# Weight loads in 8 KB doubles, the projection moved to the fifth block, and a reordered last block

## The chip, the cores and the metric

The kernel runs on one core of one Trainium2 chip. The metric is the time of one execution on the device in microseconds (us), as the median of several runs. PE is the matrix engine (PEld its weight loads), DVE the vector engine, ACT the activation engine, POOL the general-purpose engine and SP the engine whose queue issues nearly all transfers. The core has 16 DMA engines, which all queues share.

## The reference, cut to what matters

256 tokens of width 1024 pass one hybrid layer, all in 32-bit floats:

```
h = rms_norm(x); proj = h @ w_in                # 1024 x 6160
y_a = attention(q, k, v) @ w_out_a
y_b = state_space_mixer(z, xbc, dt) @ w_out_b
x = x + (gate_a * y_a + gate_b * y_b) @ w_out
h2 = rms_norm(x)
for e in 16 experts:                            # each token uses 2 of them
    he = silu(h2 @ w_gate[e]) * (h2 @ w_up[e])  # 1024 x 512 each
    x += combine[:, e] * (he @ w_down[e])       # 512 x 1024
x = x + sigmoid(x @ w_ple_gate) * (p @ w_ple_proj)
out = rms_norm(x)
```

The weights are 143.6 MB of reads in all; the experts alone hold 16 x 6 MB. Which experts serve which tokens is known only after the router has seen the normalized x.

## The kernel before, in words

**Order of the work.** The input projection, attention, the state-space mixer and the output projections come first (a list of "pieces", each with a split of a weight chunk into a high and a low part, products and an evacuation). Then the router runs (`route`, L998), and the experts are handled in six blocks (`for pr in range(NB)`, L1475): blocks 0 to 3 hold two experts with 64 slots each, blocks 4 and 5 hold four experts with 32 slots each. Experts 0 to 3 (blocks 0 and 1) are always in place, so their weights can be loaded ahead; the experts of the later blocks are taken in an order that `sort_experts` (L1061) writes into registers, and their loads wait for that. A block computes gate and up products (`gate_up`, L1151), transposes the hidden rows (`hidden_T`, L1184), multiplies by the down weights (`down`, L1190), splits the result into yh and yl and adds it back to the tokens one block later (`scatter`, L1208). `down` for the last two blocks is cut in halves and quarters of the output columns (`half_down` L1450, `q_down` L1463), so that the gate `w_ple_gate` (chunks pg_0 to pg_7, `pg_split` L1548, `pg` L1552) can begin on the first columns while the others are still loaded. From L1602 on the order of this last part is written out by hand.

**Memory.** On-chip memory is a ring of 51 units, each 1024 floats (4 KB) in each of 128 partitions (`UNITS`, L20). Activations take units (`Act`, L117; `Late` takes them on first use), and so do weights. A load is 512 KB, one unit. All loads stand in one list, `pending`, in the order of their use, and `pump` (L153) issues as many of its first entries as there is room for, always from SP's queue. `consumed` (L164) gives a weight's unit back when its last product has been issued, and pumps again. `Ring.may` (L73) is the planner: the kernel is first walked through dry, which notes every taking and giving back in program order; a load is admitted if at no point up to its own release the ring would be over-full. A unit that is reused is guarded by a wait of SP's queue on its last reader.

**Rows.** One load brings to each partition rows of contiguous memory: 4 KB for gate and up weights (`w_rows`, L226: two rows of 512 floats of the 8 that a partition holds) and for the down weights of blocks 0 to 3 (`d_rows`, L231), 2 KB for the halves of the down weights in blocks 4 and 5 (`d_half`), 1 KB for their quarters (`d_cols`) and for the input projection's chunks.

**The projection p @ w_ple_proj.** Its input `pin` (256 KB, rows of 1 KB) and its weights `pj_0`, `pj_1` (512 KB each) stand in the list behind w_out, ahead of the experts (L218). `pp_T` transposes p in the output projection's pieces, `pp_fill` strews the products over the places where PE would wait during routing and block 0, and `pp_end` (L1330) evacuates four PSUM banks into two units behind block 0's gate and up products.

Of the kernel before, what the change touches and what calls it, by code (L numbers as in the profile page):

```python
# [15 lines left out]
P = 128  # L16
# [3 lines left out]
UNITS = 51  # L20
# [32 lines left out]
class Ring:  # L53
# [19 lines left out]
    def may(self, name):  # L73
# [3 lines left out]
        if any(self.used[t] >= UNITS for t in r):  # L77
            return False
# [14 lines left out]
def emit(ctx, tc, ring, x, p, mix_norm_g, w_in, conv_w, conv_b, dt_bias,  # L93
# [12 lines left out]
    free = list(range(UNITS))  # L106
    pending, ready = [], {}
    known, regs = [], {}
    dry = ring.used is None

    def unit(name, dt=F32):
        if dry:
            return tc, 0
        i = free.pop(0)
        return big.tile([P, 1024], dt, tag=f"s{i}", name=name), i

    class Act:  # L117
        def __init__(self, name, n, dt=F32):
            ring.note(n)
            got = [unit(f"{name}{j}", dt) for j in range(n)]  # L120
            self.t = [g[0] for g in got]
            self.i = [g[1] for g in got]
# [4 lines left out]
        def free(self, fill=True):  # L127
            ring.note(-len(self.i))
            free.extend(self.i)
            if fill:  # L130
                pump()

    class Late:


        def __init__(self, name, n, dt=F32):
            self.name, self.dt, self.a = name, dt, [None] * n
            self.t = self

        def __getitem__(self, j):  # L140
            if self.a[j] is None:
                self.a[j] = Act(f"{self.name}{j}", 1, self.dt)
# [9 lines left out]

    def pump(limit=None):  # L153
        while pending and limit != 0 and (dry or known or not callable(pending[0][1])) and ring.may(pending[0][0]):
            name, src, nk = pending.pop(0)
            if callable(src) and not dry:
                src = src()
            t, i = unit(name)
            o = t[:, :512] if name == "pin" else t
            sp.dma_start(o.rearrange("p (k f) -> p k f", k=nk), src)  # L160
            ready[name] = (t if name == "pin" else t.rearrange("p (k f) -> p k f", k=nk), i)
# [56 lines left out]
    queue_proj()  # L218
# [7 lines left out]
    def w_rows(x, src, c):  # L226
        if x < FIXED:
            return dram(src, x * D * DFF + 2 * c * DFF, [[KD * DFF, P], [DFF, 2], [1, DFF]])
        return lambda: expert(x, src).rearrange("o (p k) f -> p (o k) f", p=P)[:, 2 * c:2 * c + 2, :]

    def d_rows(x, c):  # L231
        if x < FIXED:
            return rows(w_down, x * D * DFF + c * P * D, 1, D, D)
        return lambda: expert(x, w_down)[:, c * P:(c + 1) * P, :].rearrange("o p d -> p o d")

    def d_half(x, h, o):

        return lambda: expert(x, w_down).rearrange("o (k p) d -> p (o k) d", p=P)[:, 2 * h:2 * h + 2, o:o + 512]
# [1461 lines left out]
```

## Time and profile before

| what | value |
|---|---|
| time, median of 3 runs | 499.83 us (496.88 to 500.16) |
| profiled execution, its own time | 496.42 us |
| span of the profiled execution | 494.4 us |
| granted PE clock over the span | 0.979 of full speed |
| PE busy | 462.0 us (93%) |
| DVE, ACT, POOL busy | 208.5, 183.2, 122.9 us |
| DMA | 73,270 packets, 145.25 MB, mean 294 GB/s |

The span runs from the first to the last instruction of the program; the time around it is the launch. A share of the DMA engines over 1 means that packets overlap a little. "Landing" is when the last byte of a transfer is confirmed. PE's matmuls are pipelined, so a busy PE need not be at its peak.

### The profile page before, as it was taken

Reading aid. Unit: us, or ns where it says so; the run is one execution under the profiler, and the core shown is the slowest. Engines: PE = TensorE matmul, PEld = TensorE weight load, DVE = VectorE, ACT = ScalarE, POOL = GpSimd, SP = SyncE. Lnnn points to the kernel's source line nnn. Section 1 sums busy time; section 2 is a strip of 40 time slices with the busy share of each in tenths; the row PEclk is TensorE's granted clock in tenths of the full one; section 3 lists DMA queues with packets and bytes.
Section 4 is the critical chain, followed back from the end, with each engine's and each line's share of the span. In section 5 each row is a group of like instructions: output and inputs, shape, how many; then the busy total and the mean of one; then the engine's idle time right before and its main releaser. Section 6 shows DMA issues by size and latency. Waiting matters only on the chain.

```text
span 494.4 us, 8088 instructions
## 1 busy us (share of the span) xinstructions
PE 462.0 (93%) x3001; PEld 318.7 (64%) x3001; DVE 208.5 (42%) x412; ACT 183.2 (37%) x333; POOL 122.9 (25%) x82
## 2 busy tenths in 40 slices
PE   7999999999999999999999999999999598879881
PEld 6997998999988999988854354353532121236551
DVE  4424678795669584753635112010110000024345
ACT  5646576634677364443532111020110000123233
POOL 3857546333788630041400000000000000000001
PEclk8999999999999999999999999999999889999997
DMA  8899999611323698769558999999999999999902
GB/s 287 242 335 349 348 349 281 195 61 56 117 85 129 216 397 286 273 200 351 183 189 308 385 410 408 410 409 409 409 409 391 406 407 409 396 396 372 371 35 86
DMA packets 73270, 145.25 MB, mean 294 GB/s; under 512 B 8244, under 2 KB 41352, under 8 KB 73224
## 3 DMA queue, kind: packets, MB, share of 16 engines
q1 hardware_dynamic: 73080, 144.15, 81.1%
q8 instruction: 25, 0.41, 0.3%
q10 hardware_dynamic: 144, 0.52, 0.3%
q14 instruction: 21, 0.17, 0.1%
HBM read 143.61 MB, written 1.05 MB: 293 GB/s over the span
## 4 chain that ended last, share of the span: by engine, by line
PE 72%; DMA 17%; DVE 6%; ACT 2%; issue 1%; POOL 0%; POOLq 0%; DVEq 0%; SPq 0%; ACTq 0%
PE g L1168 7%; DMA u<-in_w_up_dram 6%; PE y L1198 6%; PE u L1168 6%; PE ac_gb L411 5%; PE ac_ob L411 5%; PE ac_ga L411 5%; DMA d_h<-in_w_down_dram 4%; DMA g<-in_w_gate_dram 4%; PE ac_xs L411 3%; PE ac_q L411 2%; PE ac_bc L411 2%; PE ac_z L411 2%; PE g L1111 2%; PE ac_k L411 2%; DMA pg<-in_w_ple_gate_dram 2%
## 5 line engine op out<-in xcount | busy, mean ns | idle before, releaser
L1586 POOL TENSOR_TENSOR stat<-stat,nhalf 128x1 f32<-128x1 f32 x2 | 1.6, 818 | 244.4 <-DVE stat L1581 242.5
L1168 PE MATMUL u<-u,XT 128*64 128x512 f32 (+1 forms) x256 | 55.9, 598 | 3.3 <-DMA u<-in_w_up_dram 3.2
L1168 PE MATMUL g<-g,XT 128*64 128x512 f32 (+1 forms) x256 | 50.4, 643 | 5.7 <-PEq L1245 4.6
L1168 PEld LDWEIGHTS u<-u,XT 128*64 128x64 f32 (+1 forms) x256 | 14.3, 123 | 40.5 <-issue 21.4
L1168 PEld LDWEIGHTS g<-g,XT 128*64 128x64 f32 (+1 forms) x256 | 14.6, 130 | 38.8 <-issue 31.0
L1198 PE MATMUL y<-d,mid 128*64 128x512 f32 x128 | 28.3, 595 | 0.0
L1181 DVE SCALAR_TENSOR_TENSOR mid<-u,cwt,mid 128x512 f32<-128x512 f32 x6 | 4.5, 751 | 50.7 <-issue 49.5
L380 POOL TENSOR_TENSOR wl_xs<-xs,wh_xs 128x1024 fp32r<-128x1024 f32 x8 | 19.2, 2396 | 17.7 <-ACT wh_xs L377 7.8
L1144 ACT ACTIVATE sT<-st 128x256 fp32r<-128x256 f32 x6 | 2.3, 385 | 52.9 <-DVE cwt L1143 50.5
L1205 DVE SCALAR_TENSOR_TENSOR yl<-y,cwt,yh 128x512 fp32r<-128x512 f32 x8 | 6.0, 750 | 34.0 <-ACT yh L1204 33.6
L1140 DVE COPY cwt<-st 128x1 f32<-128x1 f32 x6 | 0.9, 158 | 45.2 <-PE st L1135 45.2
L1198 PEld LDWEIGHTS y<-d,mid 128*64 128x64 f32 x128 | 8.9, 137 | 16.7 <-issue 15.4
L759 POOL TENSOR_TENSOR su<-su,su 128x768 f32<-128x768 f32 x8 | 16.9, 2109 | 7.6 <-ACT su L758 7.0
L1188 ACT ACTIVATE mid<-hT 128x512 f32<-128x512 f32 x5 | 3.0, 598 | 34.7 <-PE hT L1187 34.7
L380 POOL TENSOR_TENSOR wl_wo<-wo,wh_wo 128x1024 fp32r<-128x1024 f32 x3 | 7.8, 2615 | 31.0 <-ACT wh_wo L377 29.6
L389 PE MATMUL pg<-wh_pg,x2h 128*128 128x512 f32 x32 | 13.5, 423 | 0.7 <-ACT x2h L1543 0.7
L1204 ACT ACTIVATE yh<-y,cwt 128x512 fp32r<-128x512 f32 x8 | 5.5, 688 | 22.5 <-PE y L1198 22.5
L380 POOL TENSOR_TENSOR wl_z<-z,wh_z 128x1024 fp32r<-128x1024 f32 x4 | 9.6, 2405 | 16.3 <-ACT wh_z L377 7.1
L390 PE MATMUL pg<-wl_pg,x2h 128*128 128x512 f32 x32 | 12.9, 402 | 0.1
L391 PE MATMUL pg<-wh_pg,x2l 128*128 128x512 f32 x32 | 12.8, 401 | 0.0
L1119 ACT ACTIVATE XT<-g,gfd 128x256 f32<-128x256 f32 x12 | 5.0, 471 | 21.0 <-PE g L1111 21.0
L1111 PE MATMUL g<-S,h2h 128*128 128x256 f32 x44 | 11.5, 295 | 0.6 <-ACT XT L1119 0.6
(413 smaller groups left out, 1169.8 us busy)
## 6 DMA issues: line engine op xcount, KB each, us to landing
g<-in_w_gate_dram SPq DMA_DIRECT2D x64, 512.0 KB, 10.1
u<-in_w_up_dram SPq DMA_DIRECT2D x64, 512.0 KB, 10.1
d<-in_w_down_dram SPq DMA_DIRECT2D x40, 512.0 KB, 9.5
d_h<-in_w_down_dram SPq DMA_DIRECT2D x16, 512.0 KB, 10.4
xs<-in_w_in_dram SPq DMA_DIRECT2D x8, 512.0 KB, 8.7
z<-in_w_in_dram SPq DMA_DIRECT2D x8, 512.0 KB, 8.7
ga<-in_w_in_dram SPq DMA_DIRECT2D x8, 512.0 KB, 8.7
gb<-in_w_in_dram SPq DMA_DIRECT2D x8, 512.0 KB, 6.7
```

The lines of the kernel that those rows point to most:

```text
L380: (pool if pool_lo else dve).tensor_tensor(l, src, h.bitcast(F32), OP.subtract)
L389: pe.matmul(o, lh, rh, start=start, stop=False, skip_group_check=skip)
L390: pe.matmul(o, lh, rl, start=False, stop=False, skip_group_check=skip)
L391: pe.matmul(o, ll, rh, start=False, stop=stop, skip_group_check=skip)
L411: pe.matmul(st["b"][:, T * f:T * f + T], w[:, k, 128 * f:128 * f + 128], x_.k(kk), start=(n + kk + f == 0), stop=(n == 2 and kk == 4 * k_u ...
L759: pool.tensor_tensor(e, e, cbm[:, t // 4:t // 4 + 1, :].to_broadcast([P, 2, 384]), OP.mult)
L1111: pe.matmul(b[:, 256 * k:256 * k + 256], MO[hs, i].t[0][:, kk * P:(kk + 1) * P], S, start=(first and n == 0 and k == 0), stop=(last and n ...
L1119: act.activation(o[:, 256 * k:256 * k + 256], b[:, 256 * k:256 * k + 256], AF.Copy, scale=g2[:, k:k + 1])
L1168: pe.matmul(b[part(pr, s), :], xg.k(kk)[:, part(pr, s, s0)], ready[f"{w}{e}_{c}"][0][:, k, :], start=(kk == 0), stop=(kk == KD - 1), skip_ ...
L1198: pe.matmul(by[hf][part(pr, s), :], mo["hT"][:, c, part(pr, s)], w[:, 0, 512 * hf:512 * hf + 512], start=(c == 0), stop=(c == 3), skip_gro ...
L1204: act.activation(mo["yh"][:, sl], by[hf], AF.Copy, scale=cw)
L1205: dve.scalar_tensor_tensor(mo["yl"][:, sl], by[hf], cw, mo["yh"][:, sl].bitcast(F32), op0=OP.mult, op1=OP.subtract)
```

## The change

The ring becomes 25 doubles of 8 KB in each partition. An activation of one unit takes a half; activations of one group (`grp`) share a double, and a double is free again only when both halves are. Loads are paired in the order of the list (`pair_up`); gate and up weights and the down weights of blocks 0 to 3 fill a whole double with one load of 1 MB, whose rows are 8192 bytes. `consumed` gives a double back when both of its loads are used. For the down weights, a partition now holds neighbouring rows of the weights, so `hidden_T` transposes every second (blocks 0 to 3) or every fourth (blocks 4 and 5) column of the hidden rows.

The projection's three loads move behind the gate and up weights of block 4 (the fifth block), and all of its work becomes `pp_all`, ahead of block 4's half_down, with one PSUM bank in turn. Where `pp_fill` stood, `keep_up` issues products of the identity with x whose result nobody reads.

In the last block the products that add y to the tokens (`q_sum`) are parted from the additions (`q_x2`), and some low parts of the gate's splits come later or on POOL; the first gated piece is kept in PSUM (`pg_x3`), and one of the four stores is issued from ACT's queue.

```
-UNITS = 51
+DOUBLES = 25
...
+    class Double:
+        def __init__(self, name, dt):
+            self.n, self.t, self.i = 0, tc, 0
+            if not dry:
+                self.i = free.pop(0)
+                self.t = big.tile([P, 2048], dt, tag=f"s{self.i}", name=name)
+
+        def half(self, h):
+            self.n += 1
+            return self.t[:, 1024 * h:1024 * h + 1024]
+
+        def release(self):
+            self.n -= 1
+            if self.n == 0 and not dry:
+                free.append(self.i)
+            return self.n == 0
...
+        def __init__(self, name, n, dt=F32, grp=None):
+            grp = grp or name
+            old = halves.pop(grp, None)
+            if old is not None and old.n == 0:
+                old = None
+            ring.note((n + (old is None)) // 2)
+            self.t, self.d = [], []
+            for k in range(n):
+                d, h = (old, 1) if old is not None else (Double(f"{name}{k}", dt), 0)
+                self.t.append(d.half(h))
+                self.d.append(d)
+                old = d if h == 0 else None
+            if old is not None:
+                halves[grp] = old
...
         def free(self, fill=True):
-            ring.note(-len(self.i))
-            free.extend(self.i)
+            ring.note(-sum([d.release() for d in self.d]))
...
     def pump(limit=None):
-        while pending and limit != 0 and (dry or known or not callable(pending[0][1])) and ring.may(pending[0][0]):
-            name, src, nk = pending.pop(0)
+        while pending and limit != 0 and (dry or known or not callable(pending[0][1])):
+            name, src, nk = pending[0][:3]
+            key, h = pair[name]
+            if key not in open_:
+                if not ring.may(key):
+                    return
+                open_[key] = Double(name, F32)
+            pending.pop(0)
             if callable(src) and not dry:
...
+            d = open_[key]
+            if h is None:
+                d.n += 1
+                t = d.t
+            else:
+                t = d.half(h)
...
+    def pair_up():
+
+        left = None
+        for e in pending:
+            if len(e) > 3:
+                pair[e[0]] = e[0], None
+            elif left is None:
+                left = e[0]
+                pair[left] = left, 0
+            else:
+                pair[e[0]] = left, 1
+                left = None
...
     def consumed(name):
-        ring.note(0, name)
-        free.append(ready.pop(name)[1])
+        key = ready.pop(name)[1]
+        left[key] -= 1
+        done = left[key] == 0
+        ring.note(0, key if done else None)
+        if done:
+            open_[key].n = 1
+            open_[key].release()
...
     queue_tok("wo", w_out)
-    queue_proj()
...
-            return dram(src, x * D * DFF + 2 * c * DFF, [[KD * DFF, P], [DFF, 2], [1, DFF]])
-        return lambda: expert(x, src).rearrange("o (p k) f -> p (o k) f", p=P)[:, 2 * c:2 * c + 2, :]
+            return dram(src, x * D * DFF + 4 * c * DFF, [[KD * DFF, P], [DFF, 4], [1, DFF]])
+        return lambda: expert(x, src).rearrange("o (p k) f -> p (o k) f", p=P)[:, 4 * c:4 * c + 4, :]
...
-            return rows(w_down, x * D * DFF + c * P * D, 1, D, D)
-        return lambda: expert(x, w_down)[:, c * P:(c + 1) * P, :].rearrange("o p d -> p o d")
+            return dram(w_down, x * D * DFF + 2 * c * P * D, [[2 * D, P], [D, 2], [1, D]])
+        return lambda: expert(x, w_down)[:, 2 * c * P:2 * (c + 1) * P, :].rearrange("o (p k) d -> p (o k) d", p=P)
...
+        return lambda: expert(x, w_down).rearrange("o (p k) d -> p (o k) d", p=P)[:, 2 * h:2 * h + 2, o:o + 512]
...
+        return lambda: expert(x, w_down).rearrange("o (p k) d -> p (o k) d", p=P)[:, :, 256 * q:256 * q + 256]
+
+    def hidden(pr, k):
+        return slice(k, 512, 4) if pr >= NB - 2 else slice(256 * (k // 2) + k % 2, 256 * (k // 2) + 256, 2)
...
-            for c in range(4):
+            for c in range(2):
                 for e in members(bl):
-                    pending.append((f"{w}{e}_{c}", w_rows(e, src, c), 2))
+                    pending.append((f"{w}{e}_{c}", w_rows(e, src, c), 4, 2))
...
         else:
+            if bl == NB - 2:
+                queue_proj()
             queue_half(bl, "h", 0)
...
-                for e in members(pr):
-                    consumed(f"{w}{e}_{c}")
+                for e in members(pr) if c % 2 else ():
+                    consumed(f"{w}{e}_{c // 2}")
...
-            pe.transpose(b[:, k * P:(k + 1) * P], mo["mid"][:, k * P:(k + 1) * P], ident)
+            pe.transpose(b[:, k * P:(k + 1) * P], mo["mid"][:, hidden(pr, k)], ident)
...
+    def keep_up(n):
+
+        if "warm" not in MO:
+            MO["warm"] = bank(3, "warm2")
+        for _ in range(n):
+            pe.matmul(MO["warm"][:, 0:256], ident, xt[0][:, 0:256], start=True, stop=True, skip_group_check=True)
...
-    def pp_T():
+    def pp_all():
...
+        act.activation(pT, b.rearrange("p (k t) -> p k t", k=2), AF.Copy)
+        pp["t"] = Act("pp", 2).t
+        for i in range(2):
+            for hf in range(2):
+                b = bank(5, f"pp{i}{hf}")
...
+                    pe.matmul(b, pT[:, k, i * P:(i + 1) * P], ready[f"pj_{k}"][0][:, 0, 512 * hf:512 * hf + 512],
+                              start=(k == 0), stop=(k == 1))
+                dve.tensor_copy(pp["t"][i][:, 512 * hf:512 * hf + 512], b)
...
-    at(W + 3, pp_T)
...
             if pr == 0:
-                pp_fill(3)
+                keep_up(2)
             if i == 0:
                 hidden_T(pr, mo)
-        if pr == 0:
-            pp_end()
         if pr == NB - 2:
+            pp_all()
             half_down(pr, mo["hT"], cw, "h", 0)
         else:
...
-    def q_x2(q):
+    def q_sum(q):
...
+
+    def q_x2(q):
+        o = quarter(q % 2)
...
-    def pg_split(c):
-        pgw[c] = split(f"pg_{c}", 1) + ([],)
-        lows.pop()()
+    def pg_split(c, low=True):
+        pgw[c] = split(f"pg_{c}", 1, pool_lo=c == 0) + ([],)
+        if low:
+            lows.pop()()
...
+    def pg_x3(i, hf, j=None):
+
+        return pgb[0, 0] if (i, hf) == (0, 0) else sc.t[i][:, pg_cols(hf, j)]
...
-        dve.tensor_tensor(t, t, xt[i][:, sl], OP.add)
+        dve.tensor_tensor(pg_x3(i, hf, j), t, xt[i][:, sl], OP.add)
...
-    def store(i, h):
+    def store(i, h, q=sp):
...
-        sp.dma_start(dram(out, i * P * D + 512 * h, [[D, P], [1, 512]]), sc.t[i][:, s])
+        q.dma_start(dram(out, i * P * D + 512 * h, [[D, P], [1, 512]]), sc.t[i][:, s])
...
     half_down(NB - 1, mo["hT"], cw, "h", 0)
+    q_sum(0)
+    q_sum(1)
+    pg_split(0)
     q_x2(0)
-    pg_split(0)
     q_x2(1)
...
     half_down(NB - 2, hT_a, pend[2], "r", 1)
     pg(2, 1)
     scatter(pend[0], mo, pend[1], (0, 1), (1,))
+    q_down(2)
     pg(3, 0)
-    q_down(2)
-    pg_split(4)
-    pg(3, 1)
+    pg_split(4, False)
+    q_sum(2)
     q_x2(2)
+    lows.pop()()
+    pg(3, 1, (0,))
     q_T(2)
     pg_split(5)
+    pg(3, 1, (1,))
     pg(4, 0)
     pg(5, 0)
-    pg_split(6)
-    pg_split(7)
+    pg_split(6, False)
+    pg_split(7, False)
     q_down(3)
     pg(4, 1, (0,))
+    q_sum(3)
     q_x2(3)
+    lows.pop(0)()
     pg(4, 1, (1,))
     q_T(3)
+    lows.pop()()
     pg(5, 1, (0,))
...
-    store(1, 0)
+    store(1, 0, act)
```

## Rows read from the trace of the kernel before

**Rows 1.** Busy time by stage (the start and end of each in us; then its length, and for PE, PEld, DVE, ACT and POOL the busy us with the number of instructions; then the granted PE clock, the DMA engines' share and their GB/s).

```profile
165.00:272.00 107.00, 106.77 (x748) 88.90 (x748) 59.88 (x116) 45.00 (x72) 23.86 (x18) 1.00 0.78 273
272.00:358.00 86.00, 85.45 (x430) 37.00 (x426) 11.33 (x24) 12.43 (x24) 0.00 (x0) 1.00 1.03 406
358.00:437.80 79.80, 68.29 (x344) 17.46 (x342) 5.33 (x16) 6.56 (x12) 0.00 (x0) 0.96 1.03 402
437.80:472.60 34.80, 31.23 (x195) 19.03 (x196) 13.75 (x21) 10.95 (x16) 0.00 (x0) 0.95 1.00 358
472.60:494.40 21.80, 10.35 (x44) 7.27 (x44) 12.80 (x23) 8.23 (x19) 1.64 (x2) 0.83 0.13 49
```

**Rows 2.** The timeline of SP's queue: start, us until the last issue of the run has gone out, the transfer, how many in a row.

```profile
265.89 9.03 SPq L160 DMA_DIRECT2D g<-in_w_gate_dram  x8
275.40 7.04 SPq L160 DMA_DIRECT2D u<-in_w_up_dram  x8
283.40 9.29 SPq L160 DMA_DIRECT2D d<-in_w_down_dram  x8
293.64 10.01 SPq L160 DMA_DIRECT2D g<-in_w_gate_dram  x8
304.46 8.98 SPq L160 DMA_DIRECT2D u<-in_w_up_dram  x8
314.39 9.66 SPq L160 DMA_DIRECT2D d<-in_w_down_dram  x8
325.00 19.52 SPq L160 DMA_DIRECT2D g<-in_w_gate_dram  x16
345.47 19.98 SPq L160 DMA_DIRECT2D u<-in_w_up_dram  x16
366.40 9.52 SPq L160 DMA_DIRECT2D d_h<-in_w_down_dram  x8
376.81 19.89 SPq L160 DMA_DIRECT2D g<-in_w_gate_dram  x16
397.62 19.56 SPq L160 DMA_DIRECT2D u<-in_w_up_dram  x16
```

**Rows 3.** Busy time by stage as in rows 1, three short stretches: the first loads with rows of 1 KB only, the second nearly all with rows of 2 KB, the third with rows of 4 KB.

```profile
52.00:62.00 10.00, 10.00 (x85) 9.05 (x84) 7.00 (x18) 4.97 (x13) 4.66 (x2) 1.00 1.10 349
378.00:384.00 6.00, 5.66 (x30) 1.88 (x28) 0.03 (x1) 0.60 (x1) 0.00 (x0) 1.00 1.05 389
320.00:340.00 20.00, 20.00 (x104) 9.18 (x102) 2.97 (x5) 2.81 (x5) 0.00 (x0) 1.00 1.03 409
```

**Rows 4.** The page's packets of all transfers, by size.

```profile
DMA packets 73270, 145.25 MB, mean 294 GB/s; under 512 B 8244, under 2 KB 41352, under 8 KB 73224
```

**Rows 5.** What SP's queue waited for (us in total, times, longest us), from 240 to 262 us above the dots, from 277 to 440 us below them.

```profile
SPq L160 <- PE g L1168: 14.1, 3, 8.3
SPq L160 <- PE u L1168: 3.3, 1, 3.3
...
SPq L160 <- DMA u<-in_w_up_dram: 33.8, 48, 1.1
...
SPq L160 <- PE y L1198: 3.8, 4, 2.3
```

**Rows 6.** What PE waited for from 358 to 440 us, in the same form.

```profile
PE u L1168 <- DMA u<-in_w_up_dram: 3.2, 13, 0.3
```

**Rows 7.** The chain that ended last, in order of time (start, us, what), around block 0's products.

```profile
225.92 0.44 PE pT L1310 x4
...
268.78 1.30 PE pp L1319 x6
270.08 7.02 PE y L1198 x32
```

**Rows 8.** The instructions on the projection's tiles: durations in ns as least/median/most, first and last start in us.

```profile
L1319 PE MATMUL pp<-pj,pin x32: 377/379/483, 241.7 to 269.7; 128*128 128x256 f32 x32
...
L1338 DVE COPY pp<-pp x2: 678/679/680, 267.6 to 268.2; 128x512 f32<-128x512 f32 x2
...
L1311 ACT ACTIVATE pin<-pT x1: 579/579/579, 227.3 to 227.3; 128x512 f32<-128x512 f32 x1
```

**Rows 9.** The timeline of the last part: start, us, engine, line, operation, tiles, and in brackets the idle time before it and what ended it.

```profile
472.42 2.46 DVE L380 TENSOR_TENSOR wl_pg<-pg,wh_pg 128x1024 fp32r<-128x1024 f32 x2 [3.20 <-ACT wh_pg L377]
...
473.53 0.46 ACT L1447 ACTIVATE yh<-y,cwt 128x256 fp32r<-128x256 f32 x1
...
474.80 0.48 DVE L1448 SCALAR_TENSOR_TENSOR yl<-y,cwt,yh 128x256 fp32r<-128x256 f32 x1
...
475.75 0.75 DVE L1535 TENSOR_TENSOR x<-x,x 128x256 f32<-128x256 f32 x2 [0.48 <-PE x L1531]
...
477.75 0.69 DVE L1544 TENSOR_TENSOR x2l<-x2T,x2h 128x512 fp32r<-128x512 f32 x1 [1.25 <-ACT x2h L1543]
...
479.06 0.39 PE L390 MATMUL pg<-wl_pg,x2h 128*128 128x512 f32 x1
...
488.55 2.50 SPq L1600 DMA_DIRECT2D out_dram<-sc  x4
...
488.96 1.41 DVE L1594 SCALAR_TENSOR_TENSOR sc<-sc,stat,fng 128x512 f32<-128x512 f32 x2 [0.44 <-POOL stat L1586]
```

**Rows 10.** POOL's groups of instructions by line: busy us, mean ns of one, idle time before.

```profile
L380 POOL TENSOR_TENSOR wl_xs<-xs,wh_xs 128x1024 fp32r<-128x1024 f32 x8 | 19.2, 2396 | 17.7 <-ACT wh_xs L377 7.8 <-PE ac_xs L411 5.0 <-DMA gb<-in_w_in_dram 4.6
```

More of the change, by code (lines that the diff above doesn't have):

```diff
@@ L76, in may @@
         r = range(max(self.now - 1, 0), self.end[name])
-        if any(self.used[t] >= UNITS for t in r):
+        if any(self.used[t] >= DOUBLES for t in r):
             return False
@@ L102, in emit @@
     ctx.enter_context(tc.manual_schedule())
-    free = list(range(UNITS))
+    free = list(range(DOUBLES))
     pending, ready = [], {}
-    known, regs = [], {}
+    known, regs, halves = [], {}, {}
     dry = ring.used is None
[L111 to L115, printed above, removed]
-    class Act:
[L118 to L122, printed above, removed]
+    class Double:
[12 more added lines that the diff above has]
+            return self.n == 0
+    class Act:
+        def __init__(self, name, n, dt=F32, grp=None):
[12 more added lines that the diff above has]
+                halves[grp] = old
         def k(self, k):
@@ L133, in emit, with __init__ @@
     class Late:
[L136 to L137 removed]
+        def __init__(self, name, n, dt=F32, grp=None):
+            self.name, self.dt, self.a, self.grp = name, dt, [None] * n, grp or name
             self.t = self
@@ L141, in __getitem__ @@
             if self.a[j] is None:
-                self.a[j] = Act(f"{self.name}{j}", 1, self.dt)
+                self.a[j] = Act(f"{self.name}{j}", 1, self.dt, self.grp)
             return self.a[j].t[0]
@@ L277, in emit @@
     queue_pg(6, 7)
-    X = [Act(f"x{i}", 1) for i in range(2)]
+    left = pair_up()
+    X = [Act(f"x{i}", 1, grp="x") for i in range(2)]
     xt = [a.t[0] for a in X]
@@ L303, in emit @@
     HH, HL = Act("hh", 2, F32R), Act("hl", 2, F32R)
-    U = [Act(f"su{i}", 1) for i in range(5)]
+    U = [Act(f"su{i}", 1, grp="su") for i in range(5)]
     UR = Act("sr", 1, F32R)
@@ L374, in split @@
         f = 1024 // nk
-        wh, wl = Act(f"wh_{name}", 1, F32R), Act(f"wl_{name}", 1, F32R)
+        wh, wl = (Act(f"{n}_{name}", 1, F32R, "split") for n in ("wh", "wl"))
         h, l = (a.t[0].rearrange("p (k f) -> p k f", k=nk) for a in (wh, wl))
@@ L491, in late @@
         if n not in lazy:
-            lazy[n] = Late(n, cnt, dt)
+            lazy[n] = Late(n, cnt, dt, {"v": "vb", "bc": "vb", "yah": "ya", "yal": "ya"}.get(n))
         return lazy[n]
@@ L1192, in down @@
         if "yh" not in mo:
-            mo["yh"], mo["yl"] = (Act(n, 1, F32R).t[0] for n in ("yh", "yl"))
+            mo["yh"], mo["yl"] = (Act(n, 1, F32R, "y").t[0] for n in ("yh", "yl"))
         for c in range(4):
@@ L1196, in down @@
                 for s, e in enumerate(members(pr)):
-                    w = ready[f"d{e}_{c}"][0]
-                    pe.matmul(by[hf][part(pr, s), :], mo["hT"][:, c, part(pr, s)], w[:, 0, 512 * hf:512 * hf + 512],
+                    w = ready[f"d{e}_{c // 2}"][0]
+                    pe.matmul(by[hf][part(pr, s), :], mo["hT"][:, c, part(pr, s)], w[:, c % 2, 512 * hf:512 * hf + 512],
                               start=(c == 0), stop=(c == 3), skip_group_check=True)
-            for e in members(pr):
-                consumed(f"d{e}_{c}")
+            for e in members(pr) if c % 2 else ():
+                consumed(f"d{e}_{c // 2}")
         for hf in range(2):
```

68 lines of the change are left out of this document (23 added, 45 removed).

## The prediction, made before the changed kernel was run

> **What bounds the kernel now.** First the table by stage [rows 1]: its columns give PE's busy time and, at the end, the share and rate of the DMA engines. Up to 272 us PE is never idle while the DMA engines stand at 0.78, so PE sets the time. From 272 to 358 us both are full (PE 85.45 of 86.00 us, DMA 1.03). From 358 to 437.8 us PE has 11.5 us to spare and the DMA engines have none, and up to 472.6 us they still read 1.00. So the DMA engines never rest for the 200.6 us between 272 and 472.6; whatever lengthens or shortens that stream moves the end one for one. The last 21.8 us are a tail of arithmetic behind the last load.
>
> Then the queue that issues the loads [rows 2]: from 275 us on, eight units of 512 KB take 10.2 us, sixteen about 20.5, or 1.28 us a unit without a break. Its waits say why [rows 5]: at 240 to 262 us it waits for PE to give back weight buffers (14.1 and 3.3 us), that is, memory is full; from 277 to 440 us it waits almost only for earlier transfers (33.8 us in 48 waits for one name), hardly for PE (3.8 us in four). PE's own waits behind 358 us are for weights [rows 6]. So three things decide: the rate of the stream, its bytes, and how much is already loaded when it begins.
>
> **Rows of 8192 bytes.** The stream shows three row lengths [rows 3]: 1 KB rows run at 349 GB/s, 2 KB rows at 389, 4 KB rows at 409. A unit is 524,288 bytes, so it takes 1.502, 1.348 and 1.282 us; an engine has 32, 16 and 8 rows of it. The steps give (1.502 - 1.348)/16 = 9.6 ns and (1.348 - 1.282)/8 = 8.3 ns a row. With 8 KB rows an engine has 4 rows fewer: 4 x 9 = 0.036 us less, 1.246 us, 421 GB/s. Gate and up weights and the down weights of blocks 0 to 3 get these rows: from the issue at 265.89 us on, 8 x 6 and 16 x 4 units (the d_h loads keep 2 KB) [rows 2], 112 units, **-4.0 us**. The bounds: nothing at all, and the whole step from 2 to 4 KB again (0.066 a unit, -7.4 us). I take the per-row value, since two independent steps agree on it.
>
> The Trainium skill, page "DMA: Bandwidth & Descriptors", section "Why small descriptors are slow (HBM only)", puts the overhead at about 3 bus cycles a packet against 32 bytes a cycle. By that estimate 4 KB rows would beat 1 KB rows by 7%, where the trace shows 17%, and 8 KB rows would save 1.2%, 1.7 us instead of 4.0; the measured steps decide.
>
> **The projection's loads move into the full stream.** The 256 KB of p with 1 KB rows cost 0.75 us, two units of its weights 2 x 1.28: **+3.3 us**. They used to travel early in the stage that reads 0.78, where the DMA engines had room [rows 1]. Could the places that they leave let expert weights in earlier? Count 4 KB places at 277 us, where memory is full. Before: 51 less x 2, split activations 4, one-hot rows 1, their transposes 1, mid 1, XT 2, y 2, projection result 2, leaving 36 for weights. After: 25 doubles less x 1, split activations 2, one-hot rows with transposes 1, mid 1 (half of it empty), XT 1, y 1, leaving 18 doubles, 36 again. The places that the projection gives up go to the lost fifty-first unit and the empty half. So the full 3.3 stands; the other bound is 0.
>
> **When the stream begins.** PE now does four transposes less at 225.92 us (0.44 us), and before the first down matmul two dummy products instead of three projection products: the six records of 1.30 us become four, about 0.43 us less [rows 7]. Memory comes back so much earlier: **-0.7 us**. Against it, a double comes back only when both halves are used, so weights return in fours, every second step. The step is half of a 7.02 us group of 32 matmuls [rows 7], 3.5 us, while four units take 5.0 us to load: the queue holds work across each step. Bounds: -1.8, and +5 where four places are missing for good (4 x 1.25).
>
> **The projection in block 4.** On PE it is the 32 records it was, about 0.22 us apart, 7 us, now with one PSUM bank, so each of four pairs waits for a DVE copy (0.68 us), besides the transposes (0.44) and an ACT copy (0.58) [rows 7, 8]: about 11 us. It sits ahead of block 4's half_down, whose eight d_h loads take some 10.4 us [rows 2] after the projection's own; what half_down loses is covered by the 32 gate and up units behind it (40 us). It eats PE's slack of 11.5 us [rows 1], but the next thing PE needs arrives 20 us later. Cost 0; without that cover it would be some 5 us. Queued behind it on PE is only half_down; on DVE nothing that the stream waits for.
>
> **The last block.** pg_7's split waits for the last landing at 472.5 us. Today DVE does both low parts (2.46 us) ahead of yl at 474.80 [rows 9]. With them put off, yl starts when yh is there, 473.53 + 0.46 = 473.99. The additions (0.75 us) follow at about 474.97, then wl of chunk 6 (1.23) to 476.95, x2l (0.69) to 477.67, wl of chunk 7 (1.23) to 478.93. The product that needs it runs at 479.06 today: **-0.1 us**. What yl gains, the late split gives back. One of four stores goes to ACT: the four issues take 2.50 us from 488.55, DVE delivers the last piece at 488.96 + 1.41 = 490.37, so the last issue can be over 0.2 us sooner: **-0.2 us**. x3 kept in PSUM has equally long operations, 0. The first low part on POOL takes 2.4 us instead of DVE's 1.23 [rows 9, 10] while DVE does the additions; d_2 and d_3, which land later, hide that. Moving q_down(2) ahead makes PE wait for d_2, time it has. Bounds of all this: -1.5 and +1.
>
> The strided transposes (4 a block) and wider lumps lie beside the stream: 0. **Sum:** -4.0 + 3.3 - 0.7 - 0.3 = -1.7 us. The profiled execution took 496.42 us (span 494.4 and 2.0 around it), 3.4 below the median of the three runs, 499.83. Carried over to the median: 498.1 us.
>
> **Rivals.** (1) *The gain without the price*, 0.27: three places really hold more weights at 277 us, so the projection is free: -5.0, 494.8; with the larger row step (-7.4) 491.4. For it: two PE stages wait on memory [rows 5]. Against: the count of 36.
>
> (2) *Rows are cut at 4096 bytes*, 0.10: no packet gets longer, so the change does not do what its name says. +3.3 - 0.7 - 0.3 = 2.3, 502.1. Against: 46 of the 73,270 packets are 8 KB or longer [rows 4], though none is a row of a load. The Trainium skill, same page, section "SWDGE vs HWDGE vs iDMA", gives "≤4096 B preferably" for a packet; only if loads of this queue follow it does this case come.
>
> (3) *Slower: the queue runs dry between lumps*, 0.13. Place: block 1's down product, around 302 us, and the same spot of blocks 2 and 3. There PE does gathers and scatters and frees nothing, and the queue already waited 2.3 us for PE's y [rows 5]. If the first pair of a double no longer frees anything, the next issue comes 1.8 us later and the queue must bridge it. It decides if less than about two units are in flight then; each of three spots would cost the 2.3 us, +7 on the forecast: 505. Against: that wait left no dip in the DMA share [rows 1].
>
> **Numbers.** Forecast 498.1 us, 0.50, alone 495 to 501. Rival 1 is faster by over 1% (5 us, about what a measurement here can tell), rival 2 is no change by that bound, rival 3 slower: 0.27, 0.60, 0.13. The range leaves out the lower end of rival 1 and rival 3: 492 to 503.5.
>
> **What would show it.** Stream: sixteen units (now eight issues of 1 MB) every 19.9 us rather than 20.5, 421 GB/s between 300 and 360 us; 409 means rival 2. Packets: 160 units of 128 rows become 64, some 10,200 fewer. Projection: 3.3 us between block 4's u and d_h loads. Ring: the issue queue's wait for PE's y behind 277 us stays near 3.8 us; if it grows to 8 or more and the DMA share falls below 1.00 there, rival 3. Tail: last landing to end 21.5 us against 21.9. I am wrong if the stream's rate is outside 409 to 430, or if PE, not DMA, is what the last blocks wait for.

## The result, and the profile after

The changed kernel takes 506.32 us (median of four runs, 504.48 to 508.58); the kernel before, run beside it four times, 500.0 us (496.88 to 500.72). The ratio is 1.0143 with a 95% interval from 1.0100 to 1.0185: slower by 1.4%, outside the predicted range and on the other side. The profiled execution took 504.48 us, its span 502.4.

Three points cut both spans: the first product with w_in (ac_q, at 10.7 us before, 11.7 after), the first gate product of block 0, called the marker, and the split of the last loaded unit (wh_pg), which starts 0.02 us after the last landing. Instructions of PE on g in the kernel before, durations in ns, then first and last start:

```profile
L1168 PE MATMUL g<-g,XT x8: 592/592/643, 248.4 to 249.7; 128*64 128x512 f32 x8
```

The same in the changed kernel:

```profile
L1231 PE MATMUL g<-g,XT x8: 592/592/644, 257.3 to 258.7; 128*64 128x512 f32 x8
```

The last split in the timeline of the kernel before:

```profile
472.56 1.06 ACT L377 ACTIVATE wh_pg<-pg 128x1024 fp32r<-128x1024 f32 x1 [0.18 <-DMA pg<-in_w_ple_gate_dram]
```

and of the changed kernel:

```profile
481.16 1.06 ACT L440 ACTIVATE wh_pg<-pg 128x1024 fp32r<-128x1024 f32 x1 [0.18 <-DMA pg<-in_w_ple_gate_dram]
```

The marker comes 8.9 us later; 1.0 us of that lies before ac_q, which begins between 10.7 and 13.3 us over all the runs. From the marker to the last split it is 224.2 us before and 223.9 after; from the split to the end of the span 21.8 and 21.2. So the whole loss lies ahead of the marker, in the part for which the prediction has next to no term. By stage, in the form of [rows 1] (the same windows, though the changed kernel is some 9 us behind in all but the first):

```profile
165.00:272.00 107.00, 106.75 (x780) 92.66 (x780) 63.62 (x115) 46.59 (x74) 30.73 (x22) 1.00 0.69 264
272.00:358.00 86.00, 85.49 (x426) 37.23 (x423) 14.56 (x34) 11.27 (x22) 0.00 (x0) 1.00 1.00 412
358.00:437.80 79.80, 62.52 (x374) 20.35 (x373) 7.44 (x20) 6.81 (x13) 0.00 (x0) 0.98 1.02 412
437.80:472.60 34.80, 32.02 (x177) 16.99 (x173) 9.73 (x16) 10.38 (x15) 2.36 (x1) 0.95 1.06 384
```

This table alone would mislead: the stream is faster (412 GB/s against 406 and 402), its share still 1.00 and more. What is wrong shows only earlier. From 60 to 160 us, same columns, before:

```profile
60.00:160.00 100.00, 98.53 (x813) 92.38 (x812) 76.99 (x148) 62.49 (x126) 56.61 (x27) 1.00 0.51 164
```

and after:

```profile
60.00:160.00 100.00, 94.11 (x746) 87.94 (x743) 69.85 (x146) 56.50 (x117) 49.21 (x23) 0.97 0.41 132
```

PE idles 5.9 us instead of 1.5, its granted clock is 0.97 instead of 1.00, and it gets through 746 matmuls instead of 813. Why, the waits of ScalarE between 10 and 245 us tell: for which producer, us in total, times, longest. Before, of the waits of a split's high copy for a low part of a split:

```profile
ACT wh_gb L377 <- DVE wl_gb L380: 4.0, 1, 4.0
ACT wh_q L377 <- DVE wl_k L380: 0.5, 1, 0.5
```

After (L440 is the high copy, L443 the low part; the trace names both halves of a double after its first, so both are wh_...):

```profile
ACT wh_wo L440 <- POOL wh_wo L443: 9.0, 3, 3.2
ACT wh_gb L440 <- POOL wh_gb L443: 5.9, 2, 3.6
ACT wh_k L440 <- POOL wh_q L443: 5.9, 2, 5.1
...
ACT wh_oa L440 <- POOL wh_ga L443: 4.1, 1, 4.1
...
ACT wh_bc L440 <- POOL wh_v L443: 2.5, 1, 2.5
```

In all there are 18 such waits with 49.4 us, where there were two with 4.5. One of them stands in the chain that ended last, at 153 us (start, us, what):

```profile
153.04 2.36 POOL wh_ga L443
155.40 0.02 issue
155.42 0.95 ACT wh_oa L440
156.38 0.01 issue
156.39 0.51 ACT su L820
...
158.46 0.27 ACT su L816
158.72 0.04 issue
158.77 0.50 PE bc L810 x2
```

POOL's low part of a split of ga (2.36 us) holds the high copy of the next split, oa. Behind that copy stand, in ScalarE's order, the exponentials and scalings of the state-space scan, and PE waits 1.84 us for the last of them. The same copy and PE's product in the timeline, with the idle time before each and what ended it:

```profile
155.42 1.06 ACT L440 ACTIVATE wh_oa<-oa 128x1024 fp32r<-128x1024 f32 x1 [4.11 <-POOL wh_ga L443]
...
158.77 0.50 PE L810 MATMUL bc<-sr,identr 128*128 128x256 f32 x2 [1.84 <-ACT su L816]
```

Why should the copy of oa wait for the low part of ga? The program's own list of who holds which memory answers it. Before, a split drew two units of 4 KB: the high part's had mostly last held the low part of four splits earlier, and the unit just given back by the split before (its loaded weights) went to the low part, which is written later. After, high and low part share one double, and in long stretches every second split draws the double of the loaded pair that the low part right before it has just finished reading. Of the 68 splits ahead of the router, the high copy goes into the piece (a unit before, a double after) that the low part directly before it reads in 1 case before, and in 23 after; these counts come from the program, not from a trace. With 25 doubles full of loads there was one free double to choose from at most splits, two or more at a few.

In these 23 cases the copy waits for more than the bytes that it overwrites. By the program, the copy of oa goes into the first half of ga's double, whose last reader is the low part of the split before, on VectorE:

```profile
146.41 1.23 DVE L443 TENSOR_TENSOR wh_ga<-ga,wh_ga 128x1024 fp32r<-128x1024 f32 x1 [0.19 <-ACT wh_ga L440]
```

That was over at 147.6 us. POOL's low part, for which the copy waited until 155.4 us, reads the other half: a double comes back as a whole. So the tying of the halves, which the expectation of e1 below lists as another theory, is part of the cause. No run gave the halves back one by one.

### The profile page after: what moved, and what is told of

It is laid out like the page before. It is cut to its first block, busy times and chain, and to the rows that moved or that the text cites. A ratio compares the mean times of both kernels' runs of the same rounds, so it can differ in the third digit from the quotient of the medians.

```text
span 502.4 us, 7789 instructions
## 1 busy us (share of the span) xinstructions
PE 460.9 (92%) x3013; PEld 323.4 (64%) x3013; DVE 213.4 (42%) x413; ACT 181.1 (36%) x331; POOL 122.9 (24%) x83
## 2 busy tenths in 40 slices
DMA packets 61748, 145.23 MB, mean 289 GB/s; under 512 B 6965, under 2 KB 40073, under 8 KB 51465
## 3 DMA queue, kind: packets, MB, share of 16 engines
HBM read 143.61 MB, written 1.05 MB: 288 GB/s over the span
## 4 chain that ended last, share of the span: by engine, by line
PE 41%; DMA 20%; SPq 2%; DVE 2%; ACT 2%; issue 1%; POOL 0%; DVEq 0%; ACTq 0%
DMA u<-in_w_up_dram 7%; PE u L1231 6%; PE g L1231 6%; PE y L1261 5%; PE ac_gb L474 5%; PE ac_ob L474 5%; DMA d_h<-in_w_down_dram 4%; DMA g<-in_w_gate_dram 3%; PE g L1174 2%; SPq L194 2%; DMA d_r<-in_w_down_dram 2%; DMA d<-in_w_down_dram 2%; DMA pg<-in_w_ple_gate_dram 2%; PE warm L1368 1%; PE x L1278 1%; PE wo L453 1%
## 5 line engine op out<-in xcount | busy, mean ns | idle before, releaser
L443 POOL TENSOR_TENSOR wh_pg<-d_h,wh_pg 128x1024 fp32r<-128x1024 f32 x1 | 2.4, 2358 | 198.9 <-PE x L1580 198.9
L443 POOL TENSOR_TENSOR wh_xs<-xs,wh_xs 128x1024 fp32r<-128x1024 f32 x8 | 19.1, 2388 | 20.1 <-ACT wh_xs L440 20.1
L1268 DVE SCALAR_TENSOR_TENSOR yh<-y,cwt,yh 128x512 fp32r<-128x512 f32 x8 | 6.0, 751 | 34.6 <-ACT yh L1267 34.1
L474 PE MATMUL ac_xs<-hh,wh_xs 128*128 128x256 f32 x128 | 19.2, 296 | 0.0
L474 PE MATMUL ac_z<-hh,wh_z 128*128 128x256 f32 x128 | 18.7, 293 | 0.0
L474 PE MATMUL ac_ga<-hh,wh_ga 128*128 128x256 f32 x128 | 17.9, 283 | 0.0
L474 PEld LDWEIGHTS ac_xs<-hh,wh_xs 128*128 128x128 f32 x128 | 17.1, 199 | 1.0 <-issue 1.0
L474 PE MATMUL ac_gb<-hh,wh_gb 128*128 128x256 f32 x128 | 17.1, 284 | 0.0
L474 PEld LDWEIGHTS ac_z<-hh,wh_z 128*128 128x128 f32 x128 | 16.9, 199 | 0.1
L474 PE MATMUL ac_ob<-uh,wh_ob 128*128 128x256 f32 x128 | 16.8, 283 | 0.0
L474 PEld LDWEIGHTS ac_ga<-hh,wh_ga 128*128 128x128 f32 x128 | 16.4, 190 | 0.0
L443 POOL TENSOR_TENSOR wh_wo<-wo,wh_wo 128x1024 fp32r<-128x1024 f32 x3 | 8.6, 2869 | 30.9 <-ACT wh_wo L440 28.7
```

The costliest lines, as they stand in the source:

```text
L443: (pool if pool_lo else dve).tensor_tensor(l, src, h.bitcast(F32), OP.subtract)
L474: pe.matmul(st["b"][:, T * f:T * f + T], w[:, k, 128 * f:128 * f + 128], x_.k(kk), start=(n + kk + f == 0), stop=(n == 2 and kk == 4 * k_u ...
L1268: dve.scalar_tensor_tensor(mo["yl"][:, sl], by[hf], cw, mo["yh"][:, sl].bitcast(F32), op0=OP.mult, op1=OP.subtract)
```

## The experiments

From ac_q to the marker, ScalarE's waits of the kind shown above between 10 and 245 us (summed), marker to last landing, the bytes moved in that time and their rate, and last landing to end. Stages from one profiled execution each; ratios are medians against the kernel before on the same chip.

| kernel | ratio (95%) | ac_q to marker, us | waits, us (times) | marker to landing, us | MB, GB/s | to end, us |
|---|---|---|---|---|---|---|
| before | 1 | 237.7 | 4.5 (2) | 224.1 | 85.26, 380 | 21.9 |
| changed | 1.0143 (1.0100-1.0185) | 245.6 | 49.4 (18) | 223.8 | 87.02, 389 | 21.3 |
| e1 reserve 2 | 1.0000 (0.9974-1.0027) | 240.6 | 0 | 223.9 | 87.03, 389 | 21.3 |
| e2 before, 47 units | 1.0088 (1.0050-1.0125) | 236.8 | 4.5 (2) | 229.4 | 87.34, 381 | 21.9 |
| e3 two DMAs a double | 1.0234 (1.0180-1.0289) | 243.8 | 47.8 (18) | 228.6 | 87.03, 381 | 21.6 |
| e4 old last block | 1.0141 (1.0101-1.0181) | 246.9 | 47.3 (19) | 224.6 | 87.02, 387 | 22.5 |
| e5 before, buffers turned round | 1.0394 (1.0340-1.0448) | 257.4 | 77.6 (39) | 224.4 | 85.20, 380 | 22.2 |
| e6 reserve 1 | 1.0026 (0.9999-1.0053) | 238.9 | 6.2 (6) | 224.9 | 87.02, 387 | 21.5 |
| e7 reserve 3 | 1.0004 (0.9973-1.0035) | 238.5 | 1.4 (2) | 223.9 | 87.02, 389 | 21.3 |
| e8 reserve 1, projection early | 1.0077 (1.0051-1.0104) | 238.9 | 6.4 (6) | 225.5 | 87.80, 389 | 22.5 |
| e9 reserve 2, a double more | 0.9984 (0.9959-1.0008) | 238.1 | 0 | 223.2 | 85.98, 385 | 21.3 |
| e10 a double more | 1.0130 (1.0088-1.0172) | 246.3 | 47.4 (18) | 223.0 | 85.97, 386 | 21.3 |
| e11 before, reserve 4 units | 1.0033 (1.0002-1.0065) | 238.5 | 0.3 (1) | 223.9 | 85.24, 381 | 22.3 |

**e1: two doubles kept free until the router.**

```diff
+        self.early = 0
...
-        if any(self.used[t] >= DOUBLES for t in r):
+        if any(self.used[t] >= DOUBLES - (2 if t < self.early else 0) for t in r):
...
+    if dry:
+        ring.early = len(ring.events)
     x1_scale_end()
```

> The changed kernel, but until the router is reached the planner may fill only 23 of the 25 doubles with loads, so that a split finds a double that was given back longer ago. Marker used in all runs: the first gate product of block 0 (g<-g,XT) begins, 248.4 us before the change and 257.3 after it. Theory 1 (before the router the space is too coarse, a split gets the double that was just given back and waits for its last reader, ScalarE in order behind it, TensorE last): marker back to 249 to 253 us, time 497 to 502. Theory 2 (two halves tied together, or another edit, cost the 9 us, not the lack of space): marker stays at 256 to 258, time 504 to 508; later if the early weights now come late. Theory 3 (the price lies after the router): marker may move, the time doesn't follow.

The waits are gone and the time with them: 498.78 us, level with the kernel before in that comparison (498.32). The marker came at 253.7 us in an execution whose ac_q also began 1.4 us later; from ac_q it is 240.6 against 245.6. The loss is in the early stage, theory 3 falls.

**e2: the kernel before with less space.**

```diff
-UNITS = 51
+UNITS = 47
```

> The kernel before, with 47 units of 4 KB instead of 51, nothing else changed; the changed kernel's 25 doubles hold by my count of half-filled doubles about 46 to 47 units of data in the early stage. Theory 1: the marker goes from 248.4 to 252 to 258 us and the time to 502 to 509, the waits of ScalarE's splits on the other engines' splits appear here too. Theory 2: marker 248 to 249, time 498 to 501.

Theory 1 fell in this form: with four units less the early stage doesn't get longer (236.8 us, 4.5 us of waits). So it became theory 1b, which the program's list of holders suggests: what is dear is not the amount of space but which piece of it a split draws. Theory 2 had the marker right but not the time, 502.19 us where it allowed 498 to 501. The 0.9% come from elsewhere: four units less hold 2.1 MB less at the marker. The DMA packets from marker to last landing, before,

```profile
DMA packets 29513, 85.26 MB, mean 380 GB/s; under 512 B 2599, under 2 KB 6695, under 8 KB 29491
```

and in e2:

```profile
DMA packets 30081, 87.34 MB, mean 381 GB/s; under 512 B 2660, under 2 KB 6756, under 8 KB 30058
```

2.08 MB more at 381 GB/s are 5.5 us; 5.3 were measured (229.4 - 224.1).

**e3: the same doubles, but rows of 4096 bytes.**

```diff
-            sp.dma_start(o.rearrange("p (k f) -> p k f", k=nk), src)
+            o = o.rearrange("p (k f) -> p k f", k=nk)
+            if h is None and not dry:
+                for s in (slice(0, nk // 2), slice(nk // 2, nk)):
+                    sp.dma_start(o[:, s], src[:, s])
+            else:
+                sp.dma_start(o, src)
```

> The changed kernel, but each 1 MB load of an expert's weights is two DMAs of 512 KB with rows of 4096 bytes into the two halves of the same double; space and order are as in the changed kernel. My price for the rows is 112 units x 0.036 us = 4.0 us: marker unchanged at 257 (plus or minus 1), from the marker to the last landing 226 to 229 us instead of 223.8, time 508 to 511. If the long rows gave nothing on the path: 223 to 225 and 505 to 507. If the long rows were the cost (theory 3): time 503 or less.

The stream at full rate, in the changed kernel,

```profile
320.00:340.00 20.00, 20.00 (x106) 9.16 (x102) 1.82 (x5) 2.57 (x6) 0.00 (x0) 1.00 1.01 421
```

and in e3:

```profile
320.00:340.00 20.00, 20.00 (x104) 9.29 (x102) 1.82 (x5) 2.80 (x6) 0.00 (x0) 1.00 1.03 409
```

421 against 409 GB/s, 223.8 against 228.6 us: the long rows are worth 4.8 us, and the ratios (1.0234 and 1.0143) say about the same. They are not the cause of the loss. The edit halves the size of each DMA along with its rows, and no run parts the two; the engines' share is at 1.01 and 1.03, so no gap between DMAs shows in either kernel.

**e4: the last block as before** (additions, low parts and gate blocks in the old order, all stores on SP, no low part on POOL).

```diff
-    q_down(2)
     pg(3, 0)
-    pg_split(4, False)
+    q_down(2)
+    pg_split(4)
+    pg(3, 1)
...
-    store(1, 0, act)
+    store(1, 0)
```

> The changed kernel with the last block's additions, splits, gate blocks and the last store's queue in the order of the kernel before. My price for the new order is 0.3 us: marker 257, from the last landing to the end of the span 21.3 to 21.9 us (21.3 in the changed kernel, 21.9 before), time 506 to 507. Theory 3, if the last block were at fault: time 503 or less.

The time doesn't move (1.0141 and 1.0143), so theory 3 falls here too. The tail is longer, but e8 has 22.5 us with the new order, so one trace doesn't settle 1 us. Over all traces the new order has 21.3 to 21.6 in seven and 22.5 in one, the old one 21.9 to 22.5 in five: something like 0.6 us in favour of the new.

**e5: the kernel before, high and low buffer drawn in the other order.** Same space, same loads, same units; only which of two free units goes to which part.

```diff
-        wh, wl = Act(f"wh_{name}", 1, F32R), Act(f"wl_{name}", 1, F32R)
+        wl, wh = Act(f"wl_{name}", 1, F32R), Act(f"wh_{name}", 1, F32R)
```

> The kernel before with one line turned round: a split draws its low buffer first and its high buffer second. Space, loads and halves are as before (51 units of 4 KB), but the high copy (ScalarE) now goes mostly into the unit that the low part of the split before it gave back, where before it went into a unit from four splits ago. In the changed kernel every second split's double is of that kind. Measure: from the first product with w_in (ac_q) to the marker (first g<-g,XT), 237.7 us before and 245.6 after. Theory 1b (the cost is that the high copy must wait for the low part of the split just before it, and ScalarE in order takes the scans of attention and state space with it): 243 to 248 us, time 1 to 2% over the kernel before, waits of ScalarE wh on POOL or VectorE wl appear. Theory 2b (lack of space in doubles, or another edit): 237 to 239 us, time within 0.4% of before.

This line costs 3.9%, nearly three times the whole change. Now 51 of the 68 high copies overwrite the very unit that the low part directly before reads. ScalarE's largest waits of this kind, in the form above:

```profile
ACT wh_ga L377 <- POOL wl_ga L380: 9.3, 3, 3.4
ACT wh_ob L377 <- DVE wl_ob L380: 7.3, 5, 1.9
ACT wh_z L377 <- POOL wl_z L380: 6.8, 3, 2.6
ACT wh_wo L377 <- POOL wl_wo L380: 5.7, 2, 3.2
```

and PE's progress from 60 to 160 us:

```profile
60.00:160.00 100.00, 91.27 (x710) 84.78 (x710) 64.85 (x142) 56.17 (x115) 46.63 (x22) 0.97 0.48 149
```

The expectation took the changed kernel's cost and was too small: the dose is larger. Against the kernel before, 22 cases more go with 7.9 us (245.6 - 237.7) in the changed kernel, 50 more with 19.7 us here: 0.36 us a case at most (a part of the 7.9 may not be the waits', see e6 and e7) and 0.39. Theory 2b falls.

**e6 and e7: one or three doubles kept free**, the edit of e1 with 1 and 3.

> The changed kernel with one double kept from the loads until the router instead of two (e1 had two: 240.6 us from ac_q to the marker, time level with before). By the program's list of doubles, a split's double was then given back two splits earlier instead of one. Theory 1b: one step between is enough: 239 to 242 us, time as in e1 or up to 1 us less. If two steps are needed: 243 to 245 us, time 501 to 504.

> The changed kernel with three doubles kept from the loads until the router. Theory 1b: nothing more to gain than in e1, 239 to 241 us from ac_q to the marker; loads of the mixer's weights come later and may cost up to 2 us; from marker to last landing 224 to 226 us. If the 3 us that e1 still lacks to the kernel before (240.6 against 237.7) are also a matter of free doubles: 238 us and a time 0.5% under e1.

One double between release and use is enough: in e6 1 of 68 cases is left (the pair's double now comes two splits later), and of the waits six with 6.2 us, of which these are the longest:

```profile
ACT wh_wo L441 <- POOL wh_wo L444: 2.2, 1, 2.2
ACT wh_k L441 <- POOL wh_q L444: 1.7, 1, 1.7
```

PE from 60 to 160 us in e6:

```profile
60.00:160.00 100.00, 97.34 (x803) 90.85 (x799) 77.23 (x148) 62.28 (x126) 55.93 (x27) 1.00 0.42 132
```

e1, e6 and e7 can't be told apart (1.0000, 1.0026, 1.0004); e7's 238.5 us lie just under the 239 to 241 expected, without the 0.5% of time that the other reading of it asked for. Single traces of the early stage differ by 1 to 3 us, so take means: the five traces with a reserve (e1, e6, e7, e8, e9) have 239.0 us from ac_q to the marker, the four of the changed kernel without one (changed, e3, e4, e10) 245.7, and the kernel before with e2 and e11 237.7. Some 6.6 us of the early loss are the waits', then, and about 1.3 us stay unexplained.

**e8: the projection's loads early again**, with one double kept free.

```diff
     queue_tok("wo", w_out)
+    queue_proj()
...
-            if bl == NB - 2:
-                queue_proj()
```

> As e6, but the projection's 1 MB of loads goes back behind w_out in the order of loads; its products stay in the fifth block. My term for its place in the stream was 3.3 us: from marker to last landing 220 to 221.5 us instead of 223.8, time 2 to 3 us under e6. If the loads merely push other loads back by as much, so that the same bytes have landed at the marker: 223 to 224.5 us, time as e6.

Neither forecast came: it is not a gain but 0.5% more than e6, with 225.5 us from the marker to the landing. Although the projection's 1.31 MB are in before the marker, 87.80 MB follow it instead of 87.02: its three units occupy two doubles, and about 2.1 MB of experts' weights (0.78 + 1.31) come later for it.

**e9 and e10: one double more at the marker.** The router's table held a half-filled double; it gets 4 KB of its own.

```diff
-        MO["ca"] = Act("cmp", 1, grp="route")
+        MO["ca"] = Extra("cmp")
```

> As e1 (two doubles kept from the loads until the router), and the router's table cmp, which holds a half-filled double at the marker, gets 4 KB of its own outside the ring, so that one more 1 MB load fits before the marker. The traces so far give the time from the marker to the last landing as the bytes still to come over their mean rate: before 85.26 MB at 380 GB/s, changed kernel and e1 87.0 MB at 389, e2 87.34 MB at 381. If that is the account: 86.0 MB behind the marker (87.03 less 1.05), 221.2 us from marker to last landing instead of 223.9, time 2.5 to 2.7 us under e1's 498.8, so 496 to 497, 0.4 to 0.7% under the kernel before. If the stream is held by its lumps instead (bytes before the marker don't count): 223.5 to 224.5 us and time as in e1.

> The changed kernel with the router's table cmp in 4 KB of its own outside the ring, and nothing kept from the loads. By the account of bytes: 86.0 MB behind the marker, 221 us from marker to last landing, and from ac_q to the marker as in the changed kernel (244 to 247 us): time 503 to 504.5 us, 0.9 to 1.1% over the kernel before. If space in doubles by itself were what the early stage lacks, the marker would come earlier too: 500 us or less.

The bytes behind the marker fell by just the 1.05 MB, but the time to the last landing by 0.7 and 0.8 us, not 2.5, and e10's time (505.33 us) missed its 503 to 504.5. The packets of e9:

```profile
DMA packets 21269, 85.98 MB, mean 385 GB/s; under 512 B 1664, under 2 KB 6016, under 8 KB 13568
```

The mean rate is lower, because the stream starts slower. From 22 to 28 us after the marker, in e9:

```profile
271.00:277.00 6.00, 6.00 (x32) 2.00 (x30) 0.02 (x1) 0.69 (x1) 0.00 (x0) 1.00 0.87 315
```

and in the changed kernel:

```profile
279.30:285.30 6.00, 6.00 (x32) 2.00 (x30) 0.03 (x1) 0.69 (x1) 0.00 (x0) 1.00 0.99 380
```

The DMA engines stand idle for 13% of these 6 us, while PE is full (6.00 of 6.00). The likely reason, which no further run tests: with more loaded already, the transfers catch up with what block 0 gives back. So less space cost one for one (e2), and more space helped only as far as PE's pace through block 0 let it. In e10 the early stage is as slow as in the changed kernel: space alone doesn't cure it.

**e11: a reserve in the kernel before**, the edit of e1 with 4 of 51 units.

> Control: the kernel before with four of its 51 units (16 KB a partition, as much as two doubles) kept from the loads until the router. If the reserve helps only because it undoes what the doubles did (theory 1b; in the kernel before the high copy's unit was given back about four splits earlier anyway): from ac_q to the marker 236.5 to 238.5 us, time within 0.4% of the kernel before. If free space at the splits is worth something in any kernel: 234 to 236 us and time 0.5% or more under it.

No gain (1.0033), the early stage as good as unchanged (238.5 us against 237.7). The reserve isn't good by itself; it undoes what the doubles did.

No version beats both kernels beyond doubt: e9 beats the changed one by 1.6%, by the two ratios, and stands level with the kernel before (497.35 us against 497.79, interval across 1).

## Why the prediction was wrong

**The early stage: the step that failed.** The prediction read that up to 272 us PE is never idle and "PE sets the time", and went on to the stream. But the first of [rows 1] begins at 165 us, and by then the loss has arisen: the first product on ac_gb starts at 167.8 us before and 177.2 after, 157.1 and 165.5 us behind ac_q. Ahead of the marker the prediction had one term, the 0.44 us of the four transposes at 225.92 us, and none for the splits. It asked of the doubles only how many bytes they hold at 277 us and when block 0 gives them back. That the same doubles also serve the splits, from 10 us on, it didn't follow: the missing term is +7.9 us (245.6 - 237.7). A busy PE didn't mean that PE was safe; what feeds it is a chain through ScalarE, and [rows 10] already gave the price of one wait, POOL's low part of 2396 ns. Some 6.6 us of it are the splits' waits, and without these the kernel is level with the one before (e1, e6, e7). Even then the forecast was somewhat too good: -1.7 us is a ratio of 0.9966, and the three intervals begin at 0.9974, 0.9999 and 0.9973.

The two signs that the prediction named for being wrong, a stream outside 409 to 430 GB/s and last blocks that wait for PE, did not come (421 GB/s, and PE waits for weights, below). Both look only at the stream, so neither could show this loss.

**Rows of 8192 bytes: right.** -4.0 us forecast, 4.8 measured in e3. 421 GB/s is the rate forecast; a unit takes 524,288 bytes / 421 GB/s = 1.245 us, and the step from 1.282 is about 9 ns for each of four rows, in line with the 9.6 and 8.3 of the shorter ones. The packets:

```profile
DMA packets 61748, 145.23 MB, mean 289 GB/s; under 512 B 6965, under 2 KB 40073, under 8 KB 51465
```

11,522 fewer than in [rows 4]; some 10,200 were forecast, and 1,279 of the rest are packets under 512 B (8244 - 6965), which the forecast left out. 10,283 packets now have 8 KB or more (61748 - 51465), where 160 units of 64 rows are 10,240. So rival 2 (rows cut at 4096 bytes) falls, and with it the reading of "≤4096 B preferably" in the Trainium skill, page "DMA: Bandwidth & Descriptors", section "SWDGE vs HWDGE vs iDMA", as a limit for this queue; the sentence stands there in a table on the DMAs that GpSimd issues, and these come from SP. The estimate from the same page's section "Why small descriptors are slow (HBM only)", 1.7 us, was too small by the factor 2.8; the measured steps were the better guide.

**The projection in the stream and the earlier start: nearly right, for a reason only half right.** Forecast were +3.3 and -0.7; with the rows, and without the 0.44 us that lie ahead of the marker, that is -1.1 from the marker on. Measured were -0.3. Taking e3's 4.8 out, the rest costs 4.5 us, and the bytes give it: 87.02 - 85.26 = 1.76 MB more behind the marker, at 389 GB/s 4.5 us. Of them 1.31 MB are the projection. The other 0.45 MB are nearly one unit: at the marker the list of holders has 39 units of experts' weights and 3 of the projection's before, and 19 doubles after, 38 units. The prediction counted 36 units both before and after, at 277 us, and so saw no loss; at the marker one unit is missing. But putting the loads back early doesn't return the 3.3 us (e8): what costs is the places at the marker, not the place in the order. The 0.7 us weren't measured by themselves, so no run shows them.

**The projection in block 4: forecast 0, and no cost shows.** PE's waits from 358 to 450 us:

```profile
PE u L1231 <- DMA u<-in_w_up_dram: 8.7, 6, 1.5
...
PE pp L1387 <- DVE pp L1389: 2.4, 3, 0.8
```

PE waits for the copies as foreseen and still waits longer for weights. No run moves this work alone.

**The last block:** forecast -0.3 us, about -0.6 in the traces, not resolved in the time (e4).

**Rival 3, the queue running dry: its wait came, its price didn't.** What SP's queue waited for from 277 to 440 us, beside [rows 5]:

```profile
SPq L194 <- PE y L1261: 34.1, 8, 9.3
SPq L194 <- DMA u<-in_w_up_dram: 17.9, 11, 2.0
```

34.1 us instead of 3.8, yet the DMA share stayed at 1.00 and 1.02 (the second and third row of the table by stage): enough was in flight. Right was to ask for both signs; the slower ending came by another mechanism and some 140 us or more earlier, and that rival 3's 505 us stand close to the measured 506.32 is luck. Rival 1 (a gain without a price) falls with the 1.76 MB.

## What to carry to other kernels

Making the pieces of a buffer pool larger changes more than how much it holds: it changes which piece each writer gets, and so what it waits for. List for every writer what its buffer held before and who reads that last, in the whole piece and not only in the part that is written. Where an engine that works in order would wait for the instruction just issued elsewhere, keep one piece free, or give the fresh piece to the part that is written last. And cost a change of a shared pool in every stage that draws from it, not only in the one for which it is meant.

## What the runs showed of the hardware that was not expected

A wait of 2 to 5 us on ScalarE costs PE far less than itself, but many add up: 49.4 us in 18 waits cost at most 7.9 us, 77.6 in 39 cost 19.7. Part of it goes with the clock: from 60 to 160 us the granted clock is 1.00 before and in e6, 0.97 in the changed kernel and e5, where PE was idle 5.9 and 8.7 us of the 100. In the changed kernel it fell twice, each time behind a gap of PE, of 1.82 us (up to 78.5 us) and of 1.52 us (up to 112.8 us), to 0.50, which is the level of 1.2 GHz, and within about 4 us it rose again. Two stretches at 0.50, and the two around them:

```profile
80.00:82.00 2.00, 2.00 (x10) 1.74 (x9) 1.96 (x4) 1.27 (x4) 2.00 (x1) 0.50 0.53 183
114.00:116.00 2.00, 2.00 (x8) 1.74 (x8) 1.97 (x7) 1.48 (x3) 0.00 (x0) 0.50 0.00 0
...
78.00:83.40 5.40, 4.88 (x26) 4.06 (x27) 5.20 (x13) 3.07 (x8) 4.00 (x2) 0.68 0.57 193
112.00:117.20 5.20, 4.42 (x22) 4.19 (x23) 5.10 (x14) 2.66 (x4) 0.00 (x0) 0.67 0.21 73
```

Behind the gap of 1.84 us at 158.8 us it did not fall. Clock 0.68 and 0.67 over the two longer stretches take about 3.4 us of full-speed work (0.32 x 5.40 + 0.33 x 5.20), and PE was idle 4.4 us more than before (98.53 - 94.11). That is an estimate from one trace each, for these 100 us alone (from 10 to 60 us it is the kernel before that has 0.97, and the changed one 1.00); no run varies idle time and clock apart. The gain of longer rows goes on from 4 to 8 KB at the same 9 ns or so a row, and one core takes in 421 GB/s.
